# Cross-attention queries, keys and half the values as pairs of Strassen's seven products; recurrence spread

## The chip, the cores and the metric

The kernel runs on one core of one Trainium2 chip. The metric is the device time of one launch, in microseconds (us), as the median of several runs; a profile of one further execution shows the inside. The engines are called as the profile calls them: PE (TensorE, matrix products; PEld is its weight load), DVE (VectorE), ACT (ScalarE), POOL (GpSimd) and SP (SyncE, here a queue for DMAs).

## The reference

One decoder layer on 256 tokens of width 2048, all in float32. In short:

```python
hn = rmsnorm(h, norm_mix_w)
q, k, v, g_ret, xr, yr, g_a, g_b = split(hn @ w_in)
ret_out = silu(g_ret) * head_groupnorm(chunkwise_retention(rotary(q), rotary(k), v))
rnn_out = gelu(yr) * rg_lru(causal_dwconv(xr))        # h_t = a_t h_{t-1} + u_t
merged  = sigmoid(g_a) * (ret_out @ w_proj_ret) + sigmoid(g_b) * (rnn_out @ w_proj_rnn)
h = h + merged @ w_mix_out
hn, mem_n = rmsnorm(h, norm_xa_w), rmsnorm(mem, norm_mem_w)     # mem: 256 tokens too
q, k, v = hn @ xa_w_q, mem_n @ xa_w_k, mem_n @ xa_w_v           # 4 heads of 512
h = h + softmax(q k^T / sqrt(512)) v @ xa_w_o
h = h + (silu(gate) * val) @ ffn_w_down       # gate, val: conv(rmsnorm(h) @ ffn_w_up)
return rmsnorm(h, final_norm_w)
```

## The kernel before

**Weights.** All large products read one stream of weight pieces of 1 MiB (four tiles of 128 rows, 512 columns), listed by `weight_plan` and taken in that order by `prefetch` (line 261 issues the load on SP's queue). Each piece is split into two float32r parts: ACT copies the rounded part `hi` (L282), DVE subtracts it to get `lo` (L283). `raw` has five buffers, `hi` and `lo` three each; `AHEAD` keeps two units split ahead of the one that PE works on. Every product is then three: high by high, low by high, high by low.

**Three forms of a product.** `gemm_t` (L342) holds the weights still and streams the tokens: its result has features on the partitions, as the next stage wants it. `gemm_n` (L352 to L354) holds the tokens still and streams 512 weight columns: its result has tokens on the partitions ("by token"). `pair_products` (L380 to L383) is `gemm_n` for two adjoining blocks of 512 columns at once: of the 16 row tiles, eight are worked as 2 x 2 blocks (two token halves, even and odd row tiles, two column blocks) with the seven products of Strassen's scheme, and eight plainly. A pair has eleven units instead of eight: seven of 12 matmuls (q1 to q7) and four plain ones of 24 (p). Three of the eleven pieces are made by adding a second piece onto one that lies in SBUF, with a DMA that accumulates, issued by POOL (L263); one is made by a DVE addition (L287). The left side needs sums of the token blocks (`sums`: four DVE subtractions, then a split). Its results are gathered by `pair_out` (into new tiles) or `pair_add` (onto the residual).

**The order.** Work that hangs on a product's end is put off by `later(n, fn)`: it is written down n units further on. A scheduler then orders each engine's instructions by priority and by when it expects them to be ready, so that what is written later may stand earlier. `transposed` turns token-major tiles on PE (L480), four 128 x 128 turns at a time. `Kept` stores tiles in DRAM through POOL's queue and loads them again when they are first asked for (`kt`).

**Around the change.** `recur` (recurrence of one block of 512 channels) puts off three steps, `weigh`, `drive` and `scan`; for the last block they fall into the first pair of the gates `g_a`. The retention output `ret` is fetched from DRAM during the last blocks of `g_b` and is the left side of `w_proj_ret`. `residual` runs `w_mix_out` as one pair and two blocks, adds it to the residual (`hrow`, four tiles that stay in SBUF), and `turn` turns the new residual into the left side `h1s` of the attention. The attention then takes `gemm_t` of `xa_w_k` and `xa_w_q` for each of the four heads, `softmax` (L468) a unit later, and after that four `gemm_n` of `xa_w_v`, each followed by `attend` (L468 too). Keys are scaled by the memory's norm along the free axis (`rsb2`, made by `spread_tokens`).

Of the kernel before, what the change touches and what calls it, by code (L numbers as in the profile page):

```python
# [9 lines left out]
F32 = mybir.dt.float32  # L10
F32R = mybir.dt.float32r
I32 = mybir.dt.int32
AF = mybir.ActivationFunctionType
# [137 lines left out]
def hybrid_layer(  # L151
# [34 lines left out]
    def big(shape, dt=F32, s="b"):  # L186
        return bp.tile(shape, dt, tag="big", name=nm(s))
# [107 lines left out]
    def later(n, fn):  # L295

        pending.append((step[0] + n + 1, fn))
# [122 lines left out]

        pair_products(w, row, st, ss, c0, c1, out)

    def pair_out(w, st, ss, c0):

        o0, o1 = (big([P, 2, BW], s="o") for _ in range(2))

        def out(kind, x, z, yu, rw):
            if kind == "q1":
                act.copy(o0[:, 0, :], x)
            elif kind == "q5":  # L430
                act.copy(o1, z[:, None, :].to_broadcast([P, 2, BW]))  # L431
                later(1, lambda: dve.tensor_tensor(out=o1, in0=o1, in1=rw, op=ALU.add))
            elif kind == "q6":
                dve.tensor_tensor(out=o1[:, 0, :], in0=o1[:, 0, :], in1=x, op=ALU.subtract)
            elif kind == "q7":
                act.copy(o0[:, 1, :], x)
                dve.tensor_tensor(out=o1[:, 1, :], in0=o1[:, 1, :], in1=x, op=ALU.subtract)
            elif kind == "q4":
                dve.tensor_tensor(out=o0, in0=o0, in1=yu, op=ALU.add)

        pair_products(w, 0, st, ss, c0, c0 + BW, out)
        return o0, o1
# [119 lines left out]


    class Pairs(list):
        def __init__(self, src, wcol):
            self.src, self.wcol, self.raw = src, wcol, []

        def load(self, n):

# [11 lines left out]
        def __getitem__(self, i):  # L581
            while len(self) <= i:
                k2 = len(self)
                self.load(min(NT // 2, k2 + 2))
                self.append(split_cols(self.raw[k2], lambda j: self.wcol(2 * k2 + j)))
            return list.__getitem__(self, i)

    xs = Pairs(x_t, p_mix)
# [222 lines left out]
    def recur(b, rgw, xr, gl):  # L811
# [128 lines left out]


    hrow = [load_rows(x, c) for c in range(2)]
    ms = Pairs(mem_t, p_mem)

    def residual(w, st, ssum, out, wcol, steps=None):

        ss = sp_.tile([P, 2, 4], F32, tag="ss0", name=nm("ss"))
        for bs in ((0, 1), (2,), (3,)):
            if steps:
                steps(bs[0])  # L950
            if len(bs) > 1:
                pair_add(w, 0, st, ssum, 0, BW, hrow[0], hrow[1])
            else:
                h = hrow[bs[0]]
                dve.tensor_add(h, h, gemm_n(w, 0, st, NT, bs[0] * BW))
            for i, b in enumerate(bs):
                squares(hrow[b], ss, b)
                for pr in range(2):
                    later(2 * i + pr, lambda b=b, pr=pr: turn(b, pr, out, wcol))
        return ss  # L960

    def turn(b, pr, out, wcol):
        for t in transposed(hrow[b][:, :, pr * S : (pr + 1) * S]):
            out.append(split_cols(t, lambda j: wcol(4 * b + 2 * pr + j)))

    def squares(y, ss, i):
        for tt in range(2):
# [14 lines left out]
    def memory_rows(c):  # L982
        squares(load_rows(mem, c), ssm, c)
        if c == 3:
            rsms.append(rstd_rows(ssm))
            later(2, lambda: spread_tokens(rsms[0]))

    def memory_steps(b):
        if b == 0:
            for c in range(4):  # L990
                later(5 + 4 * c, lambda c=c: memory_rows(c))
            for c in (2, 3):
                later(1 + 4 * (c - 2), lambda c=c: hrow.append(load_rows(x, c)))
        if b == 3:
            ms.load(2)
            later(0, lambda: ms[0])
            later(1, lambda: ms[1])

    h1s = []
    ss1 = residual("w_mix_out", merged, merged_sums, h1s, p_xa, memory_steps)  # L1000


    lscale = sp_.tile([P, 2], F32, tag="ls", name="lscale")
# [47 lines left out]

    def attend(b, v):
# [22 lines left out]
    ss2 = residual("xa_w_o", osp, osp_sums, h2s, p_ffn)  # L1075
    rs2 = rstd_rows(ss2)
    later(1, lambda: spread_tokens(rs2))

# [133 lines left out]
```

## Time and profile before

| | us |
|---|---|
| median of 3 runs (lowest, highest) | 2042.58 (2040.59, 2044.53) |
| profiled execution: its time | 2039.33 |
| profiled execution: span from first to last instruction | 2037.5 |
| granted PE clock, mean | 0.998 |
| DMA moved | 424.70 MB, 208 GB/s |

A page gives each engine's busy time and share of the span. A row of a group reads: line, engine, operation, output and inputs by the program's names, count, then busy time and the mean length of one in ns, then the engine's idle time before them and what ended it. PE's matmuls overlap each other, so the mean length of one is longer than the distance between two starts; what a matmul costs is that distance.

### The profile page before, as it was taken

How to read it: one execution, taken by the hardware profiler on the slowest of the kernel's cores; microseconds unless marked ns; L12 is line 12 of the kernel's file. 1: busy time of each engine (PE TensorE's matmuls, PEld its weight loads, DVE VectorE, ACT ScalarE, POOL GpSimd, SP SyncE). 2: the span in 40 equal slices, each digit the busy share in tenths (PEclk: the TensorE clock that was granted, in tenths of full speed). 3: DMA queues.
4: the chain of work that ended last, by engine and by line, in shares of the span. 5: the costliest groups of instructions: out<-in, count | busy, mean ns of one | idle time of the engine just before them, and what ended most of it. 6: DMA issues, size and time to landing. Idle time of an engine off the chain costs nothing.

```text
span 2037.5 us, 25259 instructions
## 1 busy us (share of the span) xinstructions
PE 2015.9 (99%) x10376; PEld 1721.5 (84%) x10376; DVE 1441.1 (71%) x1483; ACT 1087.1 (53%) x1096; POOL 56.8 (3%) x81
## 2 busy tenths in 40 slices
PE   9999999999999999999999999999999999999998
PEld 8888888888787888888888888888878888788887
DVE  6747657988875777666555557587787787786775
ACT  6445446767565554465444545455554555554553
POOL 0000000000100000000000000000000000000000
PEclk9999999999999999999999999999999999999999
DMA  9554554555987785876444457455478555685552
GB/s 373 205 216 175 185 204 166 214 194 149 284 276 271 222 264 185 245 281 216 167 178 174 165 166 237 184 184 198 171 208 284 186 187 188 184 277 198 191 202 83
DMA packets 70531, 424.70 MB, mean 208 GB/s; under 512 B 7952, under 2 KB 12688, under 8 KB 22416
## 3 DMA queue, kind: packets, MB, share of 16 engines
q1 hardware_dynamic: 61264, 376.42, 50.2%
q0 software_dynamic: 7632, 44.04, 10.1%
q10 hardware_dynamic: 1520, 2.63, 0.4%
q8 instruction: 81, 1.33, 0.2%
q14 instruction: 34, 0.28, 0.0%
HBM read 416.77 MB, written 6.29 MB: 208 GB/s over the span
## 4 chain that ended last, share of the span: by engine, by line
PE 89%; DVE 4%; ACT 3%; DMA 2%; issue 1%; POOL 0%; POOLq 0%; SPq 0%; ACTq 0%; DVEq 0%
PE acc L342 43%; PE acc L352 9%; PE acc L354 9%; PE acc L353 9%; PE acc L383 6%; PE acc L380 5%; PE acc L382 5%; DVE lo L283 2%; DMA raw<-in_wall 2%; PE sm L468 2%; ACT hi L282 1%; PE sm L480 1%; DMA xt<-in_mem_t 0%; DVE fv L1088 0%; ACT tt L823 0%
## 5 line engine op out<-in xcount | busy, mean ns | idle before, releaser
L283 DVE TENSOR_TENSOR lo<-raw,hi 128x2048 fp32r<-128x2048 f32 (+1 forms) x393 | 889.0, 2268 | 466.5 <-ACT hi L282 465.6
L282 ACT CAST hi<-raw 128x2048 fp32r<-128x2048 f32 (+1 forms) x391 | 741.4, 1900 | 682.0 <-PE acc L353 189.3
L342 PE MATMUL acc<-s,hi 128*128 128x512 f32 x2688 | 641.2, 391 | 1.7 <-DVE hi L280 1.1
L342 PEld LDWEIGHTS acc<-s,hi 128*128 128x128 f32 x2688 | 496.9, 188 | 100.5 <-issue 1.6
L342 PEld LDWEIGHTS acc<-s,lo 128*128 128x128 f32 x2688 | 343.4, 191 | 12.5 <-DVE lo L283 0.9
L342 PE MATMUL acc<-s,lo 128*128 128x256 f32 x2688 | 351.0, 284 | 0.7 <-DVE lo L283 0.6
L352 PE MATMUL acc<-hi,s 128*128 128x512 f32 (+1 forms) x824 | 317.3, 386 | 0.0
L354 PE MATMUL acc<-lo,s 128*128 128x512 f32 (+1 forms) x824 | 316.1, 384 | 0.0
L353 PE MATMUL acc<-hi,s 128*128 128x512 f32 (+1 forms) x824 | 315.9, 383 | 0.0
L380 PE MATMUL acc<-hi,s 128*128 128x512 f32 x484 | 189.5, 392 | 4.5 <-ACT hi L282 3.2
L383 PE MATMUL acc<-lo,s 128*128 128x512 f32 x484 | 189.2, 391 | 0.8 <-DVE lo L283 0.5
L382 PE MATMUL acc<-hi,s 128*128 128x512 f32 x484 | 189.2, 391 | 0.3 <-DVE s L499 0.3
L354 PEld LDWEIGHTS acc<-lo,s 128*128 128x128 f32 x824 | 154.9, 188 | 31.0 <-DVE lo L283 0.2
L353 PEld LDWEIGHTS acc<-hi,s 128*128 128x128 f32 x824 | 155.0, 188 | 29.7 <-DVE s L502 0.2
L352 PEld LDWEIGHTS acc<-hi,s 128*128 128x128 f32 x824 | 154.9, 188 | 29.6 <-ACT s L501 0.3
L380 PEld LDWEIGHTS acc<-hi,s 128*128 128x128 f32 x484 | 90.9, 188 | 24.8 <-ACT hi L282 4.7
L383 PEld LDWEIGHTS acc<-lo,s 128*128 128x128 f32 x484 | 90.8, 188 | 22.3 <-DVE lo L283 3.5
L382 PEld LDWEIGHTS acc<-hi,s 128*128 128x128 f32 x484 | 90.9, 188 | 19.8 <-DVE s L499 0.8
L490 ACT COPY c<-acc 128x512 f32<-128x512 f32 x84 | 48.1, 579 | 93.0 <-PE acc L342 93.0
L383 PE MATMUL acc<-lo,ss 128*128 128x512 f32 x176 | 69.5, 395 | 2.7 <-DVE lo L283 2.7
L380 PE MATMUL acc<-hi,ss 128*128 128x512 f32 x176 | 69.7, 396 | 1.3 <-ACT o L431 1.3
L382 PE MATMUL acc<-hi,ss 128*128 128x512 f32 x176 | 69.0, 392 | 0.0
(231 smaller groups left out, 1275.3 us busy)
## 6 DMA issues: line engine op xcount, KB each, us to landing
raw<-in_wall SPq DMA_DIRECT2D x342, 1024.0 KB, 4.9
raw<-in_wall POOLq DMA_DIRECT2D x33, 1024.0 KB, 9.3
raw<-in_wall SPq DMA_DIRECT2D x5, 512.0 KB, 7.5
nat<-in_x ACTq DMA_DIRECT2D x4, 512.0 KB, 10.5
ret<-hd POOLq DMA_DIRECT2D x8, 256.0 KB, 7.4
rnn<-rn POOLq DMA_DIRECT2D x8, 256.0 KB, 4.0
kt<-ret POOLq DMA_DIRECT2D x8, 256.0 KB, 11.4
kt<-rnn POOLq DMA_DIRECT2D x8, 256.0 KB, 4.7
```

Of the source, the lines that this page charges most:

```text
L282: act.copy(hi[:, a:b], raw[:, a:b])
L283: dve.tensor_tensor(out=lo[:, a:b], in0=raw[:, a:b], in1=hi[:, a:b].bitcast(F32), op=ALU.subtract)
L342: pe.matmul(a, part, sx, start=k == 0 and t == 0, stop=k == nk - 1 and t == 0, skip_group_check=True)
L352: pe.matmul(o, h, hi, start=start, stop=False)
L353: pe.matmul(o, l, hi, start=False, stop=False)
L354: pe.matmul(o, h, lo, start=False, stop=stop)
L380: pe.matmul(o[0], h, hi, start=o[1] not in begun, stop=False, skip_group_check=True)
L382: pe.matmul(o[0], l, hi, start=False, stop=False, skip_group_check=True)
L383: pe.matmul(o[0], h, lo, start=False, stop=kk == KC - 1, skip_group_check=True)
L468: pe.matmul(o, a, b, start=start and i == 0, stop=stop and i == 2, skip_group_check=True)
L480: pe.transpose(t[:, j, tt * P : (tt + 1) * P], rows[:, tt, k + j * P : k + (j + 1) * P], ident)
L490: act.copy(c, a[:, :, S:BW])
```

## The change

1. `xa_w_q` and `xa_w_k` become two `pair_out` each (heads 0 and 1, heads 2 and 3), all queries ahead of all keys, and the first half of `xa_w_v` becomes one; its second half stays `gemm_n`.
2. Queries and keys now come by token, so they are turned on PE. The queries are copied by ACT, stored in DRAM (`Kept("qs")`) and fetched again when the keys of their head have been turned. Keys are scaled by the memory's norm as they are gathered (`pair_out` with `r`), which makes `spread_tokens` for the memory superfluous.
3. The left sides `h1s` (in `residual`) and `ms` (class `Pairs`) get sums for their first four tiles.
4. The residual `hrow` is stored in DRAM behind `w_mix_out` and fetched in four tiles after the value pair.
5. The last block's `weigh`, `drive` and `scan` are put off by 6, 11 and 17 units instead of 0, 1 and 2.
6. The fetches of `ret` are written earlier: two during the first plain block of `g_b`, four during the second, two after it.

```diff
-    plan += [(w, 0, NT, b * BW) for b in range(4) for w in ("xa_w_k", "xa_w_q")]
-    plan += [("xa_w_v", 0, NT, b * BW) for b in range(4)]
+    plan += [(w, 0, NT, b * BW, (b + 1) * BW) for w in ("xa_w_q", "xa_w_k") for b in (0, 2)]
+    plan += residual_plan("xa_w_v")
...
-        for n, fn in enumerate((weigh, drive, scan)):
+        for n, fn in zip((0, 1, 2) if b < 3 else (6, 11, 17), (weigh, drive, scan)):
             later(n, fn)
...
-        for i in range(2):
-            later(2 * i, lambda i=2 * b - 4 + i: ret[i])
+        for i in range(2 * b - 2):
+            later(i, lambda i=(i if b == 2 else i + 2): ret[i])
...
-    for i in range(KC):
-        later(i // 2, lambda i=i: ret[KC + i])
+    for i in range(6, 8):
+        later(i - 6, lambda i=i: ret[i])
...
+    hkept = dp.tile([4, P, 2, BW], F32, name="hkept")
+    for b in range(4):
+        pool.dma_start(out=hkept[b], in_=hrow[b])
...
-    for b in range(XH):
-        ks = []
-        for a in gemm_t("xa_w_k", 0, ms, NT, b * BW):
-            z = joined(a, "kz")
-            dve.tensor_tensor(out=z, in0=z, in1=rsb2, op=ALU.mult)
-            ks.append(split_pair(z))
-        qs = [split_pair(joined(a, "qz")) for a in gemm_t("xa_w_q", 0, h1s, NT, b * BW)]
-        later(0, lambda a=(qs, ks): softmax(*a))
+    qs = Kept("qs", None, False)
+
+    def keep(o, pr, kept):
+        for t in transposed(o[:, :, pr * S : (pr + 1) * S]):
+            c = tmp("qc")
+            act.copy(c, t)
+            kept.store(c)
+
+    for b in (0, 2):
+        if b == 2:
+            for i in range(KC):
+                later(2 + 2 * i, lambda i=i: ms[i])
+        for i, o in enumerate(pair_out("xa_w_q", h1s, h1s_sums, b * BW)):
+            for pr in range(2):
+                later(2 * i + pr, lambda o=o, pr=pr: keep(o, pr, qs))
+    for i in range(KC):
+        later(i // 2, lambda i=i: ms[KC + i])
+
+    def turn_key(b, o, pr, ks):
+        for t in transposed(o[:, :, pr * S : (pr + 1) * S]):
+            ks.append(split_pair(t))
+        qs[2 * b + pr]
+        if pr == 1:
+            later(1, lambda: softmax([qs[2 * b], qs[2 * b + 1]], ks))
+
+    for b in (0, 2):
+        for i, o in enumerate(pair_out("xa_w_k", ms, ms.sums, b * BW, rsms[0])):
+            ks = []
+            for pr in range(2):
+                later(3 * i + pr, lambda b=b + i, o=o, pr=pr, ks=ks: turn_key(b, o, pr, ks))
...
-    for b in range(XH):
+    for i, o in enumerate(pair_out("xa_w_v", ms, ms.sums, 0)):
+        later(3 * i, lambda b=i, o=o: attend(b, split_rows(o, rsms[0])))
+    hrow = [big([P, 2, BW], s="nat") for _ in range(4)]
+    for i in range(4):
+        pool.dma_start(out=hrow[i], in_=hkept[i])
+    for b in (2, 3):
         v = split_rows(gemm_n("xa_w_v", 0, ms, NT, b * BW), rsms[0])
         later(0, lambda b=b, v=v: attend(b, v))
```

The left sides' sums are written like this (the same in `turn`, for the first four tiles):

```diff
+                if self.summed and k2 < KC:
+                    for j in range(2):
+                        act.activation(t[:, j, :], t[:, j, :], AF.Identity, scale=self.wcol(2 * k2 + j))
+                    self.append(split_pair(t))
+                    self.sums.append(sums(t))
```

`pair_out` with a row factor `r` uses `act.mul` in place of `act.copy`, and DVE's `scalar_tensor_tensor` (with `r` or its negative `neg`) in place of the additions and subtractions, an addition of 1024 columns in two halves.

More of the change, by code (lines that the diff above doesn't have):

```diff
@@ L564, in hybrid_layer, with __init__ @@
     class Pairs(list):
-        def __init__(self, src, wcol):
+        def __init__(self, src, wcol, summed=False):
             self.src, self.wcol, self.raw = src, wcol, []
+            self.summed, self.sums = summed, []
         def load(self, n):
@@ L584, in __getitem__ @@
                 self.load(min(NT // 2, k2 + 2))
-                self.append(split_cols(self.raw[k2], lambda j: self.wcol(2 * k2 + j)))
+                t = self.raw[k2]
+                if self.summed and k2 < KC:
[3 more added lines that the diff above has]
+                    self.sums.append(sums(t))
+                else:
+                    self.append(split_cols(t, lambda j: self.wcol(2 * k2 + j)))
             return list.__getitem__(self, i)
@@ L942, in hybrid_layer, with residual @@
     hrow = [load_rows(x, c) for c in range(2)]
-    ms = Pairs(mem_t, p_mem)
-    def residual(w, st, ssum, out, wcol, steps=None):
+    ms = Pairs(mem_t, p_mem, True)
+    def residual(w, st, ssum, out, osum, wcol, steps=None):
         ss = sp_.tile([P, 2, 4], F32, tag="ss0", name=nm("ss"))
@@ L958, in residual, with turn @@
                 for pr in range(2):
-                    later(2 * i + pr, lambda b=b, pr=pr: turn(b, pr, out, wcol))
+                    later(2 * i + pr, lambda b=b, pr=pr: turn(b, pr, out, osum, wcol))
         return ss
-    def turn(b, pr, out, wcol):
+    def turn(b, pr, out, osum, wcol):
         for t in transposed(hrow[b][:, :, pr * S : (pr + 1) * S]):
-            out.append(split_cols(t, lambda j: wcol(4 * b + 2 * pr + j)))
+            if osum is not None and len(out) < KC:
+                c = tmp("tc")
+                for j in range(2):
+                    act.activation(c[:, j, :], t[:, j, :], AF.Identity, scale=wcol(4 * b + 2 * pr + j))
+                out.append(split_pair(c))
+                osum.append(sums(c))
+            else:
+                out.append(split_cols(t, lambda j: wcol(4 * b + 2 * pr + j)))
     def squares(y, ss, i):
@@ L985, in memory_rows @@
             rsms.append(rstd_rows(ssm))
-            later(2, lambda: spread_tokens(rsms[0]))
     def memory_steps(b):
@@ L993, in memory_steps @@
                 later(1 + 4 * (c - 2), lambda c=c: hrow.append(load_rows(x, c)))
[L994 to L1000, printed above, removed]
+    h1s, h1s_sums = [], []
+    ss1 = residual("w_mix_out", merged, merged_sums, h1s, h1s_sums, p_xa, memory_steps)
+    hkept = dp.tile([4, P, 2, BW], F32, name="hkept")
+    for b in range(4):
+        pool.dma_start(out=hkept[b], in_=hrow[b])
     lscale = sp_.tile([P, 2], F32, tag="ls", name="lscale")
@@ L1074, in hybrid_layer @@
     h2s = []
-    ss2 = residual("xa_w_o", osp, osp_sums, h2s, p_ffn)
+    ss2 = residual("xa_w_o", osp, osp_sums, h2s, None, p_ffn)
     rs2 = rstd_rows(ss2)
```

41 lines of the change are left out of this document (33 added, 8 removed).

## The prediction

> **What bounds the kernel now.** I read the page's table of engines first, then what PE waited for, then the chain of work that ended last.
>
> ```profile
> PE 2015.9 (99%) x10376; PEld 1721.5 (84%) x10376; DVE 1441.1 (71%) x1483; ACT 1087.1 (53%) x1096; POOL 56.8 (3%) x81
> ```
> ```profile
> PE acc L380 <- ACT hi L282: 3.2, 4, 0.9
> PE acc L383 <- DVE lo L283: 3.2, 3, 2.7
> ```
>
> The second fence gives total us, times and longest: these are the two largest of PE's waits, and together they are a third of a per cent of the span. So PE is fed nearly everywhere, and the time is the number of its instructions times the distance between their starts. DVE at 71% is the next engine, and it decides whether PE stays fed. The chain gives the distances:
>
> ```profile
> 185.79 0.87 PE sm L480 x8
> ...
> 193.07 22.24 PE acc L342 x128
> ...
> 553.94 0.50 PE acc L380
> 595.05 0.50 PE acc L380
> ...
> 1141.76 3.05 PE sm L468 x24
> 1166.60 3.01 PE sm L468 x24
> ```
>
> A unit of `gemm_t` is 32 matmuls, so four units take 22.24 us and one 5.56. The rows at 553.94 and 595.05 are the first matmuls of two pairs that follow each other with nothing between: a pair takes 41.1 us. The last two rows are the `attend` products of two heads: from one to the next pass 24.8 us, of which 3.05 are `attend`, so a `gemm_n` block of four units takes 21.8. A turn on PE takes 0.87 / 8 = 0.109.
>
> **A. PE's instruction stream.** The built order of both kernels counts it. Gone are 512 matmuls of each width on L342 (32 units: queries and keys) and 192 on L352 to L354 (two value blocks); new are 900 in pairs (five of 180) and 64 turns. Two small matmuls of `spread_tokens` go too, counted at nothing. Softmax and `attend` keep their counts.
>
> - 32 units of `gemm_t`: 32 x 5.56 = 177.9 less
> - two `gemm_n` blocks: 2 x 21.8 = 43.6 less
> - five pairs: 5 x 41.1 = 205.5 more
> - 64 turns: 64 x 0.109 = 7.0 more
>
> Sum: 9.0 less. A pair saves 3.4 us against two `gemm_t` blocks, and the sixteen turns that its results need take back 1.7; the value pair saves 2.5 and needs no turn.
>
> **B. The recurrence.** These rows of ACT, DVE and PE show where the last `weigh`, `drive` and `scan` hurt: the first pair of `g_a`.
>
> ```profile
> 496.43 1.94 ACT L282 CAST hi<-raw 128x2048 fp32r<-128x2048 f32 x1
> 498.39 1.28 ACT L833 ACT_TABLE_LOAD   x1
> 499.68 1.06 ACT L833 ACTIVATE tt<-tt 128x1024 f32<-128x1024 f32 x1
> 500.65 1.90 ACT L282 CAST hi<-raw 128x2048 fp32r<-128x2048 f32 x1
> ```
> ```profile
> 498.40 2.29 DVE L283 TENSOR_TENSOR lo<-raw,hi 128x2048 fp32r<-128x2048 f32 x1 [0.16 <-ACT hi L282]
> 500.73 2.29 DVE L287 TENSOR_TENSOR raw<-raw,raw 128x2048 f32<-128x2048 f32 x1
> 502.94 1.22 DVE L837 TENSOR_TENSOR ti<-ti,tt 128x1024 f32<-128x1024 f32 x1
> 504.07 2.28 DVE L283 TENSOR_TENSOR lo<-raw,hi 128x2048 fp32r<-128x2048 f32 x1
> 506.28 2.43 DVE L841 TENSOR_TENSOR_SCAN xr<-aa,ti 128x256 f32<-128x256 f32 x4
> ...
> 509.81 4.49 DVE L283 TENSOR_TENSOR lo<-raw,hi 128x2048 fp32r<-128x2048 f32 x2
> ```
> ```profile
> 505.98 0.50 PE L380 MATMUL acc<-hi,ss 128*128 128x512 f32 x1 [1.29 <-ACT o L431]
> ...
> 512.15 0.80 PE L383 MATMUL acc<-lo,ss 128*128 128x512 f32 x1 [2.70 <-DVE lo L283]
> ```
> ```profile
> 513.00:554.00 41.00, 40.99 (x176) 33.24 (x175) 33.83 (x33) 24.94 (x19) 5.86 (x9) 0.97 0.89 281
> ```
>
> PE is idle 1.29 + 2.70 us there, and the granted clock of the next 41 us is 0.97 (the third number from the end), some 1.2 us more: 5.2 at most can be won. In the built order `weigh` stands where it stood, ahead of q5's split; what moves is that ACT makes q2's `hi` ahead of the table load, DVE q2's `lo` ahead of L287, and `scan` goes behind q7's split. With the rows' lengths: q2 `hi` 498.4 to 500.3, its `lo` 500.7 to 503.0, L287 to 505.3, q6's `hi` (behind two copies of q5's result that PE ends at 504.3, about 1.2 us) to 507.4, its `lo` to 509.8 instead of 512.1. PE then has q2 until 506.8 and is idle about 2 us in two pieces. I take 2.0 idle and the 1.2 of clock as won: **3.2 less** (0 to 5.2).
>
> By the Trainium skill ("TensorE: Matmul & The Clock Gate", Part 1), PE's clock is halved after an idle window of about 3.4 us; in this trace idle of 1.29 and 2.70 us near each other was enough, so a new wait of that size would cost its clock too.
>
> **C. The fetch of `ret`.** The first pair of `w_proj_ret` starts on all four first tiles:
>
> ```profile
> 661.85 0.51 PE L380 MATMUL acc<-hi,s 128*128 128x512 f32 x1 [1.21 <-ACT s L498]
> 662.63 0.50 PE L382 MATMUL acc<-hi,s 128*128 128x512 f32 x1 [0.27 <-DVE s L499]
> ```
>
> In the built order their splits stand a whole unit earlier. **1.5 less** (0 to 1.5); nothing takes its place, since the piece's `hi` was ready.
>
> **D. What keeps the five new pairs fed.** Each pair has three splits and one L287 more than two plain blocks. Rows for DVE's work:
>
> ```profile
> L283 DVE TENSOR_TENSOR lo<-raw,hi 128x2048 fp32r<-128x2048 f32 x386 | 881.5, 2290 | 465.2 <-ACT hi L282 464.4
> L499 DVE TENSOR_TENSOR s<-kt,s 128x512 fp32r<-128x512 f32 x8 | 5.3, 685 | 0.0
> L451 DVE TENSOR_TENSOR sm<-xt 128x128 f32<-128x128 f32 x4 | 1.1, 285 | 0.0
> ```
> ```profile
> 554.00:595.00 41.00, 41.00 (x180) 33.65 (x180) 30.41 (x17) 25.12 (x19) 2.59 (x3) 1.00 0.86 257
> 682.00:723.00 41.00, 40.99 (x181) 33.60 (x181) 32.59 (x19) 22.75 (x15) 2.62 (x3) 1.00 0.85 255
> 1480.00:1524.00 44.00, 41.99 (x185) 33.43 (x184) 35.70 (x32) 25.26 (x20) 1.75 (x2) 1.00 0.67 202
> ```
>
> The windows give busy us of PE, PEld, DVE, ACT and POOL, then clock, DMA share and GB/s. In the first two, pairs run with PE never idle at 30 to 33 us of DVE; in the third (the first pair of `ffn_w_down`) PE is idle 2.0 of 44.
>
> *DVE.* The fullest new pair is the second of the queries: about 31 us for a pair with its gathering, and four tiles of `ms` at 2 x 0.685 + 4 x 0.285 = 2.5, so 41 us in the 42.8 that PE takes with sixteen turns. The splits are two units ahead, and counted unit by unit each still ends before its matmuls. ACT has 35 us at most. In the key pairs PE takes 3.5 us of softmax for two of the heads each, and DVE has room. *First query pair:* the last residual block is turned one unit ahead of its use, and half of its split stands behind L287: +0.5 (0 to 2.3, one L287). *First key pair:* the turns wait for the last addition of the queries, behind a split: +1 (0 to 2.3, one split).
>
> *DMA.* The residual goes out and comes back (8 x 512 KB), the queries too (16 x 256 KB), all on POOL's queue together with the accumulating loads.
>
> ```profile
> q1 hardware_dynamic: 61264, 376.42, 50.2%
> q0 software_dynamic: 7632, 44.04, 10.1%
> ```
> ```profile
> raw<-in_wall POOLq DMA_DIRECT2D x33, 1024.0 KB, 9.3
> ...
> kt<-ret POOLq DMA_DIRECT2D x8, 256.0 KB, 11.4
> ```
> ```profile
> L263 POOL DMA_DIRECT2D raw<-in_wall x33: 848/870/924, 474.9 to 1808.9; - x33
> ```
> ```profile
> DMA to landing us min/median/max: 2.9/8.6/13.8
> ```
>
> Plain loads take 0.502 x 2037.5 / 376.42 = 2.7 us of all sixteen engines per MB, 0.7 per 256 KB. A pair needs 0.85 x 41 = 34.9 us. The second query pair carries nine small transfers more and the first key pair ten: 41 to 42 us in 42.8. No pair window shows more than 0.89, so I count +1 for each (0 to 4.4: 42 / 0.89 - 42.8). The accumulating loads have slack: the page's 9.3 us stands against some 14 between their issue and their split.
>
> *The last query fetch of a pair* is queued on POOL behind q4's accumulating load, and that one behind q6's split; its softmax stands in PE's order right behind q6, and behind it the rest of the pair. After q6's `lo` PE has some 10 us of work; the fetch needs 0.9 + 0.7 on POOL, 8.6 to land (the last fence: `kt`), 0.6 on ACT and 0.7 on DVE: 11.5. Such a fetch stands in the second key pair and in the value pair: +1 each (0 to 6.7 each, with the landing of 13.8).
>
> The Trainium skill ("SBUF — State Buffer", Who interferes with whom) speaks against more work for POOL: DVE instructions in a two-port mode lock POOL out while they last, and its descriptors wait. The trace does not show it: the accumulating loads' issues take 848 to 924 ns (fence above), though DVE is busy 71% of the time.
>
> **Sum.** 9.0 + 3.2 + 1.5 = 13.7 less, and 0.5 + 1 + 2 + 2 = 5.5 more: 8.2 less. The profiled execution took 2039.33, so 2031.1 on its scale. The runs' median stands 3.3 above it: 2042.6 - 8.2 = **2034.4**.
>
> **Rivals.** *The pairs fill the DMA engines.* If 0.89 is their limit, the second query and first key pair lose 4.4 each, and the first query pair, with three or four stores of 512 KB (5 us, 40 / 0.89 against 42), 3: 11.8 instead of 2, so 13.7 less and 15.3 more: 2044. For it: no window above 0.89. Against: the window with 0.89 had PE busy throughout.
>
> *Slower: the softmax waits in PE's queue.* If the last query fetch lands after 13.8 us in both places, each waits 6.7, and the clock falls each time as at 512 (1.2): 15.8 instead of 2. With the DMA rival's other waits at half (8): 13.7 less, 24 more: 2053. It decides from a landing of about 7 us on; below it the wait is hidden. For it: 11.4 for `kt<-ret`. Against: `kt` as a whole has 8.6, and the two value or key units split ahead go on.
>
> *The recurrence is not spread.* Since `weigh` stays ahead of q5's split, B may give nothing: 2037.6.
>
> **How the numbers follow.** The forecast has 0.62, the recurrence rival 0.08, the DMA rival 0.18, the slower one 0.12. A measurement tells 0.2% from no change, 4.1 us: 2038.5 to 2046.7 is the same. The forecast and the recurrence rival lie below it but for a tenth of the forecast (waits at half their bounds), the DMA rival in it: faster 0.68, the same 0.20, slower 0.12. The range runs from all gains with no wait (9.0 + 5.2 + 1.5 less: 2027) to the DMA rival with 2 us of the queue's waits (2046); beyond lie the rest of the slower case and chance.
>
> **What would show it.** In the changed profile: two turns ahead of each key head and pair starts 42 to 43 us apart for queries; no row like 661.85; an idle PE near 507 of some 2 us, with clock 1.00 after; DMA shares of 0.9 or more in the query and key pairs; a wait of PE's L496 for L527 in the second key pair. I am wrong if the pair starts are 46 us or more apart, or if L496 waits for more than 5 us in all.

## The result

The changed kernel takes 2062.31 us (median of 4 runs, 2058.05 to 2066.09) against 2041.63 for the kernel before (now 4 runs, 2040.59 to 2044.53): a ratio of 1.0098, 95% interval 1.0075 to 1.0121. It is 1% slower; 2034.4 was forecast, with a range up to 2046. The profiled execution took 2058.05, the lowest of the four; its span is 2056.2, 18.7 more than before, at a granted clock of 0.991 (before 0.998).

First the engines on the page of the changed kernel; then, from the view of its DMAs, POOL's queue with its share of the 16 engines and two rows of issues (the last number is the median us from issue to landing).

```profile
PE 2018.2 (98%) x10120; PEld 1708.9 (83%) x10120; DVE 1496.6 (73%) x1535; ACT 1128.1 (55%) x1143; POOL 83.0 (4%) x120
```
```profile
q0 software_dynamic: 12224, 68.16, 15.3%
...
raw<-in_wall POOLq DMA_DIRECT2D x48, 1024.0 KB, 9.3
...
kt<-qs POOLq DMA_DIRECT2D x8, 256.0 KB, 12.1
```

PE has 256 matmuls fewer and yet is busy 2.3 us longer: part of its work ran at half clock. What it waited for (total us, times, longest):

```profile
PE sm L496 <- ACT s L526: 9.6, 2, 5.3
PE acc L383 <- DVE lo L283: 5.0, 6, 2.1
PE acc L380 <- ACT hi L282: 4.5, 6, 1.1
PE sm L508 <- DVE o L438: 1.9, 1, 1.9
PE acc L380 <- ACT s L552: 1.5, 1, 1.5
PE acc L380 <- DVE o L448: 1.5, 1, 1.5
PE acc L382 <- DVE s L553: 1.1, 1, 1.1
```

The first row is new: the products of a softmax (L496) wait twice for the split of a fetched query tile (L526). The last four are new too. Measured from the first matmul of a stage to the first of the next, in us:

| stage | before | after |
|---|---|---|
| three pairs of `g_a`, `g_b` | 133.11 | 135.09 |
| pairs of `w_proj_ret` | 84.27 | 81.88 |
| attention: queries to values | 290.03 | 307.88 |

The other stages differ by 1.0 or less each. So the loss lies in attention, 17.85. Its five pairs, from start to start (busy us of PE, PEld, DVE, ACT, POOL, then clock, DMA share, GB/s):

```profile
921.00:964.00 43.00, 42.62 (x190) 34.30 (x189) 30.53 (x22) 25.41 (x24) 3.93 (x5) 1.00 0.73 234
964.00:1007.70 43.70, 43.05 (x198) 35.12 (x197) 36.94 (x39) 31.18 (x34) 4.03 (x6) 1.00 0.94 289
1007.70:1061.40 53.70, 48.93 (x198) 38.62 (x197) 35.81 (x28) 29.85 (x30) 7.33 (x11) 0.87 0.79 249
1061.40:1118.60 57.20, 52.44 (x254) 43.85 (x253) 38.83 (x37) 30.55 (x34) 4.81 (x7) 0.94 0.68 203
1118.60:1176.20 57.60, 52.13 (x252) 43.48 (x252) 39.04 (x37) 30.42 (x35) 4.43 (x7) 0.94 0.75 226
```

The two query pairs take 43.0 and 43.8, within 1 us of the forecast (42.8). The first key pair, the second and the value pair lose 4.8 to 5.5 us each to waiting, and then the clock: 0.13 x 53.7 + 0.06 x 57.2 + 0.06 x 57.6 = 13.9 us. The chain of waits (start, length, what) names what came last in each:

```profile
981.65 11.42 DMA xt<-in_mem_t
...
1011.14 9.59 DMA xt<-in_mem_t
...
1083.26 0.56 POOL raw L263
1083.82 12.95 DMA kt<-qs
1096.80 0.63 ACT s L526
1097.47 4.51 PE sm L496 x18
...
1140.44 0.55 POOL raw L263
1140.99 13.62 DMA kt<-qs
1154.64 0.63 ACT s L526
```

Transfers in all of them: the memory's tiles in the second query and first key pair, and twice the last query tile of a head, issued on POOL right behind an accumulating load. Around the first of these two, in windows of 4 us:

```profile
1076.00:1080.00 4.00, 4.00 (x25) 3.48 (x24) 3.78 (x2) 1.37 (x1) 0.84 (x1) 1.00 0.29 27
...
1084.00:1088.00 4.00, 4.00 (x21) 3.32 (x20) 2.19 (x4) 3.31 (x6) 2.02 (x5) 1.00 1.03 303
1088.00:1092.00 4.00, 3.59 (x18) 2.62 (x17) 2.77 (x6) 1.32 (x3) 0.32 (x1) 1.00 1.01 223
1092.00:1096.00 4.00, 1.12 (x8) 0.85 (x6) 0.00 (x0) 0.00 (x0) 0.00 (x0) 0.94 1.01 356
1096.00:1100.00 4.00, 2.53 (x10) 2.31 (x11) 2.11 (x3) 3.20 (x4) 0.00 (x0) 0.50 0.60 238
1100.00:1104.00 4.00, 4.00 (x19) 3.60 (x18) 4.00 (x4) 1.50 (x1) 0.00 (x0) 0.71 0.29 88
```

The DMA share (before the last number) goes from 0.29 to 1.0 and stays there for 12 us while PE runs dry. The pair as a whole has only 0.68. Clock: 4 x (0.06 + 0.50 + 0.29) = 3.4 us are lost behind this one wait of 4.35 us.

The gates' pairs show the other loss. The stall near 507 is smaller, as forecast, and a new one stands at 532 and 537:

```profile
507.97 0.50 PE L380 MATMUL acc<-hi,ss 128*128 128x512 f32 x1 [0.25 <-ACT hi L282]
509.76 0.50 PE L380 MATMUL acc<-hi,s 128*128 128x512 f32 x1 [1.06 <-ACT hi L282]
...
532.03 0.61 PE L383 MATMUL acc<-lo,s 128*128 128x512 f32 x1 [2.08 <-DVE lo L283]
...
537.67 0.50 PE L380 MATMUL acc<-hi,s 128*128 128x512 f32 x1 [1.49 <-DVE o L448]
```

### The profile page after: what moved, and what is told of

Read it like the earlier page. It is cut to its first block, busy times and chain, and to the rows that moved or that the text cites. A ratio compares the mean times of both kernels' runs of the same rounds, so it can differ in the third digit from the quotient of the medians.

```text
span 2056.2 us, 24973 instructions
## 1 busy us (share of the span) xinstructions
PE 2018.2 (98%) x10120; PEld 1708.9 (83%) x10120; DVE 1496.6 (73%) x1535; ACT 1128.1 (55%) x1143; POOL 83.0 (4%) x120
## 3 DMA queue, kind: packets, MB, share of 16 engines
q0 software_dynamic: 12224, 68.16, 15.3%
## 4 chain that ended last, share of the span: by engine, by line
PE 84%; DVE 5%; DMA 5%; ACT 3%; issue 2%; POOL 0%; SPq 0%; POOLq 0%; DVEq 0%; ACTq 0%
PE acc L342 34%; PE acc L354 8%; PE acc L352 8%; PE acc L353 8%; PE acc L383 8%; PE acc L380 8%; PE acc L382 8%; DVE lo L283 3%; DMA raw<-in_wall 2%; PE sm L496 2%; ACT hi L282 1%; DMA xt<-in_mem_t 1%; DMA kt<-qs 1%; PE sm L508 1%; DVE raw L287 0%
## 5 line engine op out<-in xcount | busy, mean ns | idle before, releaser
L342 PE MATMUL acc<-s,hi 128*128 128x512 f32 x2176 | 520.0, 392 | 1.5 <-DVE hi L280 0.9
L342 PEld LDWEIGHTS acc<-s,hi 128*128 128x128 f32 x2176 | 402.5, 189 | 81.6 <-issue 1.4
L352 PE MATMUL acc<-hi,s 128*128 128x512 f32 (+1 forms) x760 | 292.6, 385 | 0.0
L353 PE MATMUL acc<-hi,s 128*128 128x512 f32 (+1 forms) x760 | 291.1, 383 | 0.0
L342 PEld LDWEIGHTS acc<-s,lo 128*128 128x128 f32 x2176 | 278.4, 192 | 11.0 <-DVE lo L283 1.9
L380 PE MATMUL acc<-hi,s 128*128 128x512 f32 x704 | 279.2, 397 | 7.3 <-ACT hi L282 4.3
L342 PE MATMUL acc<-s,lo 128*128 128x256 f32 x2176 | 284.3, 284 | 1.1 <-DVE lo L283 1.1
L383 PE MATMUL acc<-lo,s 128*128 128x512 f32 x704 | 278.3, 395 | 5.2 <-DVE lo L283 5.0
L382 PE MATMUL acc<-hi,s 128*128 128x512 f32 x704 | 278.1, 395 | 1.1 <-DVE s L553 1.1
L353 PEld LDWEIGHTS acc<-hi,s 128*128 128x128 f32 x760 | 143.0, 188 | 27.2 <-DVE s L530 0.2
L352 PEld LDWEIGHTS acc<-hi,s 128*128 128x128 f32 x760 | 143.0, 188 | 27.0 <-ACT s L529 0.3
L380 PEld LDWEIGHTS acc<-hi,s 128*128 128x128 f32 x704 | 133.9, 190 | 37.4 <-ACT hi L282 6.2
L383 PEld LDWEIGHTS acc<-lo,s 128*128 128x128 f32 x704 | 134.0, 190 | 36.9 <-DVE lo L283 9.6
L382 PEld LDWEIGHTS acc<-hi,s 128*128 128x128 f32 x704 | 134.0, 190 | 30.0 <-DVE s L553 1.9
L380 PE MATMUL acc<-hi,ss 128*128 128x512 f32 x256 | 101.7, 397 | 0.9 <-ACT o L434 0.4
L382 PE MATMUL acc<-hi,ss 128*128 128x512 f32 x256 | 99.9, 390 | 0.0
L263 POOL DMA_DIRECT2D raw<-in_wall x48 | 41.9, 873 | 1086.3 <-DVE lo L283 765.8
```

Of the source, the lines that this page charges most:

```text
L263: pool.dma_start(out=raw, in_=src, accum_op=ALU.add)
L342: pe.matmul(a, part, sx, start=k == 0 and t == 0, stop=k == nk - 1 and t == 0, skip_group_check=True)
L352: pe.matmul(o, h, hi, start=start, stop=False)
L353: pe.matmul(o, l, hi, start=False, stop=False)
L380: pe.matmul(o[0], h, hi, start=o[1] not in begun, stop=False, skip_group_check=True)
L382: pe.matmul(o[0], l, hi, start=False, stop=False, skip_group_check=True)
```

## The experiments

Each is set against runs of the kernel before on the same chip; these have medians from 2040.5 to 2042.1 us, so a difference between two runs on different chips is uncertain by about 1 us. Where only "attention" or "the gates' pairs" is given, it is the length of that stage in the profile, as in the table above. Attention's length scatters by some 3 us between runs whose attention is written alike: 307.9 in the changed kernel, 311.0 in `rec_back`, which differs from it in the recurrence alone.

**The query fetches.** Theory: the two waits of L496 come from the late fetch, and the fetch is late because of where it is issued.

```diff
+            qs.load(2 * b + 4)      # fetch_early: issue four fetches behind a key pair's last unit
...
-                pool.dma_start(out=t, in_=self.rows[len(self)])
+                (pool if self.summed else act).dma_start(...)      # fetch_act: queries on ACT's queue
```

> The changed kernel with one edit: the four fetches of turned queries that the key heads of a pair need are issued together, right behind the pair's last unit, so ahead of the next pair's accumulating loads on POOL's queue; their splits stay where they are. Theory (queue): in the changed kernel PE waits 4.4 and 5.3 us for the last query tile of the second and the fourth head, because that fetch stands on POOL behind q4's accumulating load, and each wait is followed by 6.8 us at half clock, 3.4 us of time. Without it both waits and both stretches of half clock go: 2 x 3.4 + 9.7 = 16.5 us less, 2062 becomes about 2046, and no wait of L496 for L526 above 0.5 us. Rival (the DMA engines are full in the key pairs): the fetches land as late or other loads do, PE waits elsewhere in the same pairs, and less than 5 us is won. Rival (the splits of keys and queries are late on DVE): L496 then waits for L527 and half of it, 8 us, stays.

Measured: 2048.78 us, 1.0027 (1.0016 to 1.0038), 13.5 less than the changed kernel. Both waits of L496 are gone; the second key pair takes 50.2 us instead of 57.1, and from the value pair to the end of attention 102.6 instead of 110.4. So the two fetches cost 14.7 us. The second query pair lost more in this run (48.3 us for 43.8), so attention fell by 10.9 only.

The fetches themselves got no faster. Their median landing is 12.8 us (12.1 in the changed kernel), and the four issued between 1089.1 and 1093.7 us take 15.5 to 18.4. The engines are as full as before, and for longer: in five windows of 4 us from 1089 to 1109 their share is 1.01 to 1.03, and PE is busy all but 0.41 us of these 20. What changed is the lead: the last of the four is issued at 1093.7 us and its split starts at 1144.4.

> The changed kernel with the eight fetches of turned queries issued on ACT's queue instead of POOL's, at the place in the program where they were written. In its built order the last fetch of a head stands on ACT behind the split of the head's last turned key tile, about 5 us later than POOL issues it in the changed kernel. Theory (queue): what makes a fetch land 12 to 13 us after its issue is the accumulating load of 1 MB ahead of it in the same queue; on a queue of its own 256 KB land in 3 to 5 us, so the tile is there at about the same time or 3 us sooner, and the two waits shrink from 4.4 and 5.3 to 1 to 4 us each. Rival (the DMA engines are full): the landing stays at 9 to 13 us on any queue, and with the later issue the waits grow to about 9 us each.

Measured: 2061.97 us, 1.0096 (1.0079 to 1.0113): no gain; L496 waits 5.4 and 4.4 us. The fetch of the second head's last tile (ACT's queue, then ACT's split of it), and the median landing of all eight:

```profile
1089.46 0.33 ACTq L718 DMA_DIRECT2D kt<-qs  x1
...
1101.78 0.62 ACT L526 CAST s<-kt 128x512 fp32r<-128x512 f32 x1 [6.70 <-DMA kt<-qs]
```
```profile
kt<-qs ACTq DMA_DIRECT2D x8, 256.0 KB, 4.0
```

At least half of the fetches land in 4.0 us or less, but the one that counts takes 12.3, nearly as on POOL's queue (13.0), with the engines full again (share 0.99 to 1.04 from 1090 to 1102 us). As an account of the landing time, the queue theory fell here: not the queue but what else the sixteen engines have to do at that moment makes the landing long. The Trainium skill says the same ("DMA: Bandwidth & Descriptors", Issuing engines are not separate DMA queues): the queues share the same 16 engines. The runs agree, with 12.3 us on one queue and 13.0 on the other. This run leaves the time of issue as late as it was (1089.5 us here, 1083.8 in the changed kernel), so it doesn't test what an earlier issue is worth; `fetch_early` does.

**The memory's tiles and the values.**

```diff
-        if b == 2:
-            for i in range(KC):
-                later(2 + 2 * i, lambda i=i: ms[i])
+        if b == 0:
+            ms.load(2)                                # mem_early; fetch_mem_early: ms.load(3)
+        else:
+            later(6, lambda: ms.load(NT // 2))        # fetch_mem_early: ms.load(6) at 0, the rest at 5
+        for i in range(2):
+            later(6 - b + 2 * i, lambda i=i + b: ms[i])   # fetch_mem_early: 5 - b + 2 * i
```

> The changed kernel with the memory's tiles fetched and split earlier: the first two during the first query pair instead of the second, the next two in the second at later(4) and later(6), and the loads of the last four ahead of the key pair's weight pieces on SP's queue. Theory: the waits at the start of the first key pair (996 to 1021 us: 0.65 for lo, 1.89 for the queries' last addition on DVE, 1.07 and 1.53 for the splits of the memory's fifth and later tiles, which SP fetched behind three weight pieces) and the 13.7 us at half clock that follow go, as far as they come from the crowding of DVE in the second query pair and from the late loads: 5 + 6.8, 9 to 12 us less. Rival (the turns of the second pair's queries alone hold PE up, behind the additions): 1.9 us of wait stays, and with it 3.4 us of clock; 4 to 6 us less. Rival (DMA engines full): nothing is won, the waits move into the first query pair.

Measured: 2057.76 us, 1.0069 (1.0051 to 1.0088), 4.5 less: the rival's size, but not for its reason. A memory tile is still late, and ACT stands idle 5.97 us before its scaling, with the weight splits behind it in ACT's order:

```profile
997.57 0.91 ACT L617 ACTIVATE xt<-xt,pb 128x256 f32<-128x256 f32 x2 [5.97 <-DMA xt<-in_mem_t]
```

> The edit of fetch_early, and the memory's tiles loaded earlier still: three at the start of the first query pair, three at the start of the second, the last two from its sixth unit on; the first two are split in the first query pair, the next two in the second. Theory (late memory loads): in fetch_early attention still takes 297.0 us, against some 281 for its instructions alone. In mem_early ACT stands idle 5.97 us for a memory tile in the second query pair, with the weight splits behind it in its queue, and from there DVE and PE are late up to the first key pair. With the tiles there in time the waits of 3.9, 1.5 and 3.7 us and the 10.2 us at half clock go but for about one wait of 2 us for the queries' last addition: attention 283 to 286 us, 2048.8 becomes about 2036 to 2038. Rival (DVE is simply full with the sums and splits in the second query pair): 4 to 5 us less, as mem_early, 2044.

Measured: 2038.52 us, 0.9985 (0.9975 to 0.9994). That is 10.3 less than `fetch_early`, or 9.1 with each set against the kernel before on its chip, as the late loads would have it. Attention takes 289.63 (7.4 less than in `fetch_early`), where 283 to 286 were expected, since 6.7 us of small waits and 1.7 of clock stay.

> The changed kernel with the first half of the values as two plain blocks again, as before. PE's instructions then take 2.5 us more. Theory (burst): the fourth head's last query fetch waited because it was issued together with q4's accumulating load of the value pair, in a burst that fills all DMA engines (share 1.0 from 1084 to 1096 us in the pair before); plain blocks have no accumulating loads, so the fetch lands in time, the fourth head's wait of 5.3 us and its 3.4 us of clock go, the second head's stay: 2.5 - 8.7 = 6 us less, about 2056. Rival (the splits of keys and queries are late whatever the load): both waits stay, 2.5 us more, 2065.

Measured: 2052.55 us, 1.0052 (1.0035 to 1.0068); attention 302.6, 5.3 less in spite of the longer instruction stream. L496 waits once, 4.4 us, instead of twice. The fourth head's fetch is in time, as expected, but not for the expected reason. POOL's rows for its issue, in the changed kernel (first fence, behind the value pair's accumulating load) and here (the second of the two):

```profile
1140.44 0.86 POOL L263 DMA_DIRECT2D raw<-in_wall  x1 [4.19 <-DVE lo L283]
1140.99 0.88 POOL L718 DMA_DIRECT2D kt<-qs  x1
```
```profile
1089.72 1.07 POOL L718 DMA_DIRECT2D kt<-qs  x2 [1.79 <-issue]
```

Without accumulating loads ahead of it in POOL's order, the fetch is issued 51 us earlier. It still takes 11.8 us to land, for 13.6. So the order on POOL sets when the fetch is issued, the load of the DMA engines sets how long it then takes, and the wait needs both.

**The recurrence.**

```diff
-        for n, fn in zip((0, 1, 2) if b < 3 else (6, 11, 17), (weigh, drive, scan)):
+        for n, fn in enumerate((weigh, drive, scan)):     # rec_back, fetch_mem_rec; before_spread: the reverse
```

> The changed kernel with the last block's weigh, drive and scan put off by 0, 1 and 2 units again, as before. Theory (spreading moves the stall): in the changed kernel PE waits at 508, 530 and 536 us instead of at 504 and 509, with the same 3.4 us at half clock, and the three pairs take 2.0 us more than before; undone, 2 us less than the changed kernel, within 1. Rival (the step B of the prediction: the spread does win some 3 us, and something else there lost 5): 3 us more.

> The kernel before with one line of the change alone: weigh, drive and scan of the last block put off by 6, 11 and 17 units. Theory (the spread moves the stall and adds to it): the pairs of g_a and g_b take 135 to 137 us instead of 133.1, the time is 2 to 4 us more, about 2045. By step B of the prediction: 3.2 us less, 2039. In either case the difference shows in the length of that stage in the profile rather than in the medians.

> fetch_mem_early and the recurrence put off by 0, 1 and 2 units as before. In rec_back the three pairs of the gates took 133.15 us, as before (133.11), in the kernels with the spread 135.0 to 136.9. So 2 to 3.8 us less than fetch_mem_early: about 2034, 0.4% below the kernel before. Rival (DVE full): 2041, the same as the kernel before.

Measured: `rec_back` 2059.84 us, 1.0088 (1.0066 to 1.0109), gates' pairs 133.15; `before_spread` 2043.90, 1.0018 (1.0008 to 1.0027), gates' pairs 134.86; `fetch_mem_rec` 2037.15, 0.9980 (0.9971 to 0.9990), gates' pairs 133.36. The spread costs 1.9 us of the gates' pairs in the changed kernel, 1.8 in the kernel before and 1.2 in `fetch_mem_early` (134.5 there). Why: the first fetch of `ret` stands on POOL behind the store of `scan`'s result. Before (first fence) and after:

```profile
504.32 0.87 POOL L682 DMA_DIRECT2D kt<-ret  x1
```
```profile
523.11 0.58 POOL L711 DMA_DIRECT2D rnn<-rn  x1 [11.50 <-DVE rn L883]
523.68 0.57 POOL L718 DMA_DIRECT2D kt<-ret  x1
```
```profile
529.08 0.29 DVE L479 TENSOR_TENSOR sm<-kt 128x128 f32<-128x128 f32 x1 [1.59 <-DMA kt<-ret]
...
534.32 0.29 DVE L479 TENSOR_TENSOR sm<-kt 128x128 f32<-128x128 f32 x1 [2.14 <-DMA kt<-ret]
```

The fetch is 19 us later than before, DVE stands for it (last fence, after), and `lo` stands behind.

```diff
+    ret.load(3)                                            # ret_early_spread, ret_early_012 (0, 1, 2)
     for c, b in ((O_GA, 0), (O_GA, 2), (O_GB, 0)):
```

> fetch_mem_early (with the spread of 6, 11, 17 units) and one line more: the first three fetches of ret are issued ahead of the gates' first pair, so ahead of the stores of scan's result on POOL's queue. Theory (the late fetch makes the new stall at 530 to 537): with the fetches there in time DVE does not stand for them, no weight split is late in the second pair, and what the spread saves at 507 (3.99 us idle with 0, 1, 2, 1.3 with the spread, 1.7 of clock) stays: the gates' pairs take 129 to 131 us, against 134.5 in fetch_mem_early and 133.1 before; 2038.5 becomes about 2034. Rival (a DMA burst or DVE's load makes the second stall whatever the queue): 133 to 135 us, no gain.

> ret_early_spread with the recurrence put off by 0, 1 and 2 units: the early fetches of ret alone. Theory: in the kernel before these fetches were in time already, and the stall at 504 to 512 comes from weigh, drive and scan; so 133 us as in fetch_mem_rec (133.4), and the difference to ret_early_spread, 2 to 4 us, is what the spread is worth when it delays no fetch. Rival: if both take the same, the spread is worth nothing.

Measured: `ret_early_spread` 2039.76 us, 0.9991 (0.9981 to 1.0001), gates' pairs 135.19: the theory of one late fetch fell. `ret_early_012` 2037.59, 0.9975 (0.9964 to 0.9985), gates' pairs 132.68. In `ret_early_spread` DVE stands only for the fourth tile of `ret` (1.48 us), but ACT stands for a weight piece:

```profile
522.11 5.52 ACT L282 CAST hi<-raw 128x2048 fp32r<-128x2048 f32 x3 [3.18 <-DMA raw<-in_wall]
```

**Trying for more.** `fetch_mem4_turn` is `fetch_mem_rec` with `ms.load(4)` for `ms.load(3)` and the turns of the queries at `later(3 + 2 * i + pr, ...)`; `fetch_mem4_turn_357` has 3, 5, 7 for 6, 11, 17 besides.

> fetch_mem_rec with two more edits: all four of the memory's first tiles are loaded ahead of the first query pair (there three), and the turns of a query pair's result are written three units later. In fetch_mem_rec attention took 288.3 us, of them 7.1 in gaps between PE's matmuls: 1.46 and 1.92 at 983 to 988 us, after ACT stood idle 6.97 us for the fourth memory tile with the weight splits behind it, and 1.57 and 1.66 at 1012 to 1014, where the third and fourth turn waited for ACT's copies of the first two. Theory (each wait has its cause in that queue's order, and PE's instructions alone take 281 us): both go, attention 282 to 284 us, 2037.2 becomes 2032 to 2033. Rival (DVE is full in the second query pair): the wait at 983 stays in size, somewhere in that pair, and only 3 us are won, 2034.

> The same, with the last block's weigh, drive and scan put off by 3, 5 and 7 units (in the change 6, 11 and 17, before 0, 1 and 2). In the changed kernel the spread takes away most of the stall near 507 us (3.99 us idle before, 1.31 after) and makes a new one in the next pair, at 530 to 537: the first fetch of ret stands on POOL behind the store of scan's result, at 523.7 us instead of 504.3, and DVE stands 1.6 and 2.1 us for it with a weight split behind. Theory (the late fetch makes the new stall): with scan ten units earlier the store and the fetch come earlier, and the gates' pairs take 130 to 132 us, against 133.1 with 0, 1, 2 and 135.1 with 6, 11, 17; 1 to 3 us less than fetch_mem4_turn. Rival (any spread only trades one stall for another): 133 to 135 us, no gain.

Measured: 2038.47 us, 0.9988 (0.9979 to 0.9998), attention 289.78; and 2040.45, 1.0001 (0.9991 to 1.0010), gates' pairs 138.49. Neither gained on `fetch_mem_rec`: the waits at 983 went, and others of 0.8 to 2.9 us came. With 3, 5, 7 `scan` stood in DVE's order where it stands with 6, 11, 17 (at 519 us), so that run did not test what it was meant to.

**The DMA engines alone.** All instructions and their order on each engine stay as they are; only the accumulating loads become plain. These kernels leave out the additions of weight pieces, so they show what the additions cost and are no versions to use.

```diff
-                    pool.dma_start(out=raw, in_=src, accum_op=ALU.add)
+                    pool.dma_start(out=raw, in_=src)
```

> The changed kernel with the 48 accumulating loads on POOL's queue made plain loads of the same 1 MB (the additions of weight pieces that they make are left out; all instructions, their order and the bytes fetched from the weights stay). Theory (bursts of the DMA engines): less of the engines' time per load, so the query fetches land in under 9 us and the waits of L496 for them, 9.6 us in two in the changed kernel, shrink to 4 us or less in all, and the 6.8 us of clock behind them go too; the weight pieces at 515 to 522 us come in time, and the gates' pairs take 130 to 132 us, against 135.1. Together 12 to 18 us less: 2044 to 2050. Rival (the order of the work on DVE, ACT and POOL makes the waits): nothing of it moves by more than 1 us, 2060 to 2063.

> The kernel before with its 33 accumulating loads made plain, in the same way. Theory: its stall at 504 to 512 us (3.99 us of waiting, 1.7 of clock) comes from weigh, drive and scan on DVE and ACT, and no other pair waits for a load; so it stays, 133 us for the gates' pairs and 2040 to 2042 in all. Rival (that stall is a late load as well): the gates' pairs take 129 us or less, 2036.

Measured: the changed kernel 2031.89 us, 0.9952 (0.9935 to 0.9969), 30.4 less; the kernel before 2037.45, 0.9974 (0.9965 to 0.9984), 4.6 less (1.9 between the spans of the profiled executions), with the gates' pairs at 133.10: its stall there stays, as expected, though the time moved more than that. Of `after_plain_loads`: POOL's queue and its loads, two of its waits of PE, and its first and second key pair:

```profile
q0 software_dynamic: 12224, 68.16, 9.2%
...
raw<-in_wall POOLq DMA_DIRECT2D x48, 1024.0 KB, 5.2
```
```profile
PE acc L380 <- DVE o L448: 3.1, 1, 3.1
PE sm L508 <- ACT qc L1088: 1.6, 2, 1.3
```
```profile
1005.40:1052.30 46.90, 44.24 (x193) 35.50 (x192) 33.00 (x26) 27.77 (x27) 5.08 (x10) 0.96 0.76 279
1052.30:1102.50 50.20, 49.79 (x254) 41.70 (x253) 38.73 (x37) 30.34 (x34) 4.08 (x8) 1.00 0.63 231
```

The windows' edges are rough; from first matmul to first matmul the first key pair takes 48.1 us. L496 waits for no query tile any more (they land in 6.6 to 9.0 us), and attention takes 286.74 us instead of 307.88, with the same instructions in the same order. So 21 of its 26 lost us hang on the accumulation: on the engines' time that it takes and on its own later landing, which this run does not tell apart. The price of accumulating: 15.3% of 2056.2 less 9.2% of 2030.3 us, over 48 loads, is 2.7 us of all engines each, about as much again as the load itself. The gates' pairs, however, take 134.15; here the weights are in time and DVE stands for `ret`:

```profile
525.51 0.29 DVE L479 TENSOR_TENSOR sm<-kt 128x128 f32<-128x128 f32 x1 [3.22 <-DMA kt<-ret]
...
530.78 0.29 DVE L479 TENSOR_TENSOR sm<-kt 128x128 f32<-128x128 f32 x1 [2.17 <-DMA kt<-ret]
```

The last run has both cures, with `ret.load(4)` and `fetch_early`'s edit:

> after_plain_loads (additions of weight pieces by DMA left out) with the first four fetches of ret issued ahead of the gates' first pair, and the query fetches early as in fetch_early. Theory (two late transfers, each enough by itself, make the stall at 530 us): with both in time the gates' pairs take 129 to 131 us, against 134.15 in after_plain_loads and 133.1 before and in before_plain_loads, and the time falls by 3 to 5 us, to 2027 to 2029. Rival (the order of DVE's own work makes it): 133 to 135 us, and 2031.

Measured: 2026.93 us, 0.9931 (0.9915 to 0.9948), gates' pairs 130.33, attention 285.29. PE's longest waits that are left:

```profile
PE acc L380 <- ACT hi L282: 4.8, 6, 1.1
PE sm L508 <- ACT qc L1096: 1.6, 2, 1.3
```

So two late transfers made the new stall: the tiles of `ret` behind the store, and weight pieces in a burst. With only one of them mended most of it stays (135.19 and 134.15 against 130.33), though in `ret_early_spread` the fourth tile of `ret` was late too.

## Why the prediction was wrong

**A, PE's stream: right.** Attention takes 285.3 us in `plain_loads_ret_early`, of which 3.7 are waits: 281.6, against 289.9 before, counted in the same way. That is 8.3 less; forecast were 9.0. The first query pair took 43.0 for 42.8. One reading in the step is off without harm: the rows at 553.94 and 595.05 are the first matmuls of q6 in two pairs, not of the pairs, which start at 531.87 and 573.11; the distance is a pair's either way.

**B, the recurrence: sign wrong, +2.0 for -3.2.** The step looked at the first pair of `g_a` and at DVE's and ACT's order, and there it held (idle 1.31 us for 3.99). It missed that `scan` also stores, on POOL, ahead of `ret`'s fetches, and that the next pair's weights come in a burst. With both out of the way the spread is worth up to 133.1 - 130.3 = 2.8, of which the early fetches alone give 0.4 to 0.7 (`ret_early_012`).

**C, the fetch of `ret`: right, undersized.** 2.4 less for 1.5: more than the idle time of the quoted rows went. Around them the starts of three matmuls stand 1.60, 0.78 and 0.34 us apart, where 0.23 is usual: 2.0 us, of which the rows show 1.48 as idle.

**D, the new waits: this step failed, 26 for 5.5** (307.9 - 281.6). The first query pair's +0.5 did not come. The *last query fetch* was put at +1 in each place. The path was right: behind q4's accumulating load on POOL, with the softmax in front of the rest of the pair. The landing was mis-sized: 8.6 us, the median of all earlier `kt` fetches, where these two took 13.0 and 13.6, because they are issued together with a load of 1 MB that accumulates, other fetches and weight pieces. By the step's own sum a landing of 13.0 to 13.6 makes a wait of 5.9 to 6.5; 4.4 and 5.3 were measured, and the clock behind each wait was not in the sum at all. Together they cost 6.9 and 7.8, 14.7 for 2; `fetch_early` and `values_plain` show it by taking away the lateness. The *first key pair* was put at +2 with its DMAs; it took 53.7 for 42.8, of which the clock made 7. The loads of the memory's tiles, late on SP's queue, were not in the sum; `fetch_mem_early` shows an earlier start of them to be worth 7 us of attention, 9 in the medians. The *DMA* step used mean shares of a pair: the second query pair ran at 0.94, above the 0.89 that I took for a possible limit, with PE busy all but 0.65 us, and the second key pair waited at a mean of 0.68. What counts is a stretch of 12 us at 1.0 that falls on a transfer with no lead. The *DVE* step, with 41 us for the second query pair, was too high: 36.9 were measured.

Between the two profiled executions the steps then add up: -8.3 of A, +2.0 of B, -2.4 of C and +26.3 of D are 17.6 of the 18.7 us; the rest lies in other stages.

**The rivals.** The slower one (0.12) named the mechanism and both places: 6.7 us of waiting each was too much (4.4 and 5.3), 1.2 of clock too little (3.4 each), together 16.4 for 15.8. That the totals are so close is luck; the two errors cancel. The DMA rival had the right resource and a mean for its measure. Neither had the memory's tiles or the cost of the spread, and the result lies above even 2053. "The recurrence is not spread" did not hold: it was, and cost. Both signs of being wrong came true: the two key pairs start 53.7 us apart, more than the 46 that were named, and L496 waits for 9.6 us, more than 5. The chances of the time do not follow from those of the cases as stated: with a tenth of the forecast in the middle they give 0.64 and 0.24, not 0.68 and 0.20.

**The clock.** The prediction took 1.2 us for a wait's clock, from a mean of 0.97 over a window that begins at 513; the stretch at half clock began at 511.8 and cost 1.7. The trace's record of the granted clock has stretches at half in steps of 3.41 us: one in the kernel before, and 3.41, 13.65, 6.83 and 6.83 in the changed kernel, 15.4 us lost in all (a further one at the very end of each, when PE has finished, is left out). The Trainium skill ("TensorE: Matmul & The Clock Gate", Part 1) gives a window of 3413 ns; the steps agree.

**A version that beats both.** `fetch_mem_rec` and `ret_early_012` take 0.9980 and 0.9975 of the kernel before, 4 to 5 us less, once the new transfers are issued early and the recurrence is left alone. But 2.4 of this are the earlier fetch of `ret` (step C). Attention takes 288.3 and 289.1 us, for 290.0 before: the pairs for queries, keys and values gain 1 to 2 us so far, of the 8 that their instructions would allow.

## What to carry to other kernels

A transfer's landing time is not a property of its size or queue (256 KB on ACT's queue took 4.0 us as a median, and 12.3 when it mattered): price a new fetch by what the DMA engines carry in the 10 us after its issue, in windows of a few us, not by the median landing or the mean share of a stage. Then give it a lead longer than the longest landing. In `fetch_early` the fetches took up to 18.4 us, longer than those that cost a wait, and nothing waited. Look for what stands ahead of it on the same queue, since that decides when it is issued. And when a step is put off, list its stores as well, with everything that stands behind them on the same queue.

## What the runs showed of the hardware

- A load of 1 MB that adds onto SBUF takes the 16 engines some 2.7 us more than a plain one, which takes 2.9 (estimated from 9.2% of 2030.3 us for 68.16 MB in `after_plain_loads`), and lands in 9.3 us instead of 5.2; its issue on POOL takes 868 ns instead of 540. Making 48 of them plain, and nothing else, moved the kernel by 30 us.
- Waits of PE of 4.4 to 5.8 us were followed by 6.83 us at half clock in eight of nine cases (`after`, `rec_back`, `mem_early`, `values_plain` and one in `fetch_act`); after the other one in `fetch_act`, of 4.4, it was 3.41. Waits of 1.9, 1.1 and 1.5 us within 11 us went with 13.65: short waits near each other can cost more clock than one long one. It is no fixed price: waits of 1.3 and 1.2 us, 2 us apart, cost none in `fetch_mem_rec` and 3.41 at half clock in `fetch_mem_early`.
